# SiLU as one ScalarE function in a gated-DeltaNet layer, in place of a Tanh and a VectorE combination

## The chip, the cores and the metric

The program runs on one core of a Trainium2 chip. A core has five engines that run their own instruction streams and meet through semaphores: TensorE (PE, matrix products, with its weight loads shown as PEld), VectorE (DVE), ScalarE (ACT), GpSimd (POOL) and SyncE (SP, which issues the transfers). The metric is the device time of one execution in microseconds (us); the median of three runs stands for a kernel.

## The reference, cut to what matters

The program is a trunk of four layers on 256 frames of width 1024. The mixers are, in order, gated DeltaNet (GDN), mLSTM, differential attention, and GDN again; each is followed by a squared-ReLU MLP. So the part that is changed runs twice, in layer 0 and in layer 3. In the GDN mixer SiLU stands at two places:

```python
def gdn_mixer(h, w_in, conv_w, a_log, dt_bias, norm_g, w_out):
    proj = h @ w_in
    qkv = jax.nn.silu(causal_conv(proj[..., :GDN_QKV], conv_w))
    z = proj[..., GDN_QKV:GDN_QKV + GDN_HEADS * GDN_DV].reshape(b, t, GDN_HEADS, GDN_DV)
    ...
    q = l2_norm(qkv[..., :hk].reshape(b, t, GDN_HEADS, GDN_DK))
    k = l2_norm(qkv[..., hk:2 * hk].reshape(b, t, GDN_HEADS, GDN_DK))
    v = qkv[..., 2 * hk:].reshape(b, t, GDN_HEADS, GDN_DV)
    g = -jnp.exp(a_log) * jax.nn.softplus(a + dt_bias)
    beta = jax.nn.sigmoid(bt)
    o = gated_delta_rule(q, k, v, g, beta)
    o = rms_norm(o, norm_g) * jax.nn.silu(z)
    return o.reshape(b, t, GDN_HEADS * GDN_DV) @ w_out
```

The gated delta rule solves, for each head and each block of tokens, a lower triangular system whose matrix comes from the products of the keys and from decays exp(g_i - g_j).

## The kernel before

Products are done in two parts: each weight chunk is split into a high part (ACT copies it, L160) and a low part (DVE or POOL subtracts, L166), and each product is three matmuls. All products are recorded on one line, L174, so tiles are told apart by name. For the GDN layers POOL does the subtractions for the weights of q, v and z (`wlo_g`, `wlo_gz`) and of the output (`wlo_wo_g`), one piece of 128 x 1024 at a time.

A GDN layer goes through these stages. The keys are projected by token (`gkt`), transposed (`gp_1q`), convolved over four taps (L1033 on ACT for the last tap, L1039 on DVE for three) and given their SiLU, two heads at a time: q = 0 and 1 fill `gkT0`, q = 2 and 3 fill `gkT1`. The kernel holds twice the SiLU, y (1 + tanh(y / 2)): ACT computes the Tanh into a tile `cth` (L1041), DVE combines (L1042). Meanwhile the decays are made: ACT takes absolute differences (L1077) and an Exp in place (L1082) for half the heads at a time (`Eup0`, then `Eup1`), and POOL selects the triangles from them (L1083 into `L`, L1084 in place). Then come the Gram matrices of the keys (`gG`, on PE), their diagonals on DVE (L1099, the sums into `gck`), the scaling of `L` (L1108), and a copy of its diagonal blocks into `Lc` (L1112), once for each half of the heads. When both halves are there, DVE inverts all the blocks of 32 in a long chain of small products and subtractions (`LT` L1120, `Xt` L1130, `Xb` L1134) that ends in two transposes (`Xc` L1135, `Yc` L1136). PE takes `Yc` up at L1139 (`Za`) and builds larger inverses; the solve (`gw`), the state, the update of the right sides (`grhs`, L1234), attention and output follow. The values (`cy_2q`) and queries (`gqT`) have their convolution and SiLU at L1039 to L1044, and the gate (`zg`) its own at L990 and L991.

PE's order is written by hand in this part: blocks of projections (`gp`, `gz`) are issued between the chain's products for set amounts of time (the table `FILL`), and PE then runs in that order. The orders of the other engines come from a scheduler, which orders each engine's queue; a queue runs in order, so an instruction that waits holds up all that stand behind it on its engine. The tag `cvt` has four buffers, which the `cth`, `cy` and `diag` tiles share.

ScalarE's functions come in sets of tables, and an instruction that needs a function outside the loaded set is preceded in the program by an `ACT_TABLE_LOAD`. The program before has one, at its start.

Of the kernel before, what the change touches and what calls it, by code (L numbers as in the profile page):

```python
# [45 lines left out]
def shape_constants():  # L46
    """Arrays that depend on the shapes alone."""
# [6 lines left out]
    # [(b, d, n), j, r] is 1 at r = 2 j + d  # L54
# [12 lines left out]
def trunk_kernel(  # L67
# [33 lines left out]
    def bank(name):  # L101
        """for the wide products"""
        return ps_mm.tile([P, 512], F32, tag="mm", name=name)

    def tbank(name):
        """for transposes and the mixers' small products"""
        return ps_tr.tile([P, 512], F32, tag="tr", name=name)
# [23 lines left out]
    hold, hold_early = [], []  # L131
    # the latest instructions by name of the chain of norms between two sublayers
# [8 lines left out]
    def load_w(src, a, b, name, pool=(), early=(), chained=False, after=None):  # L141
        """A chunk of a weight matrix, [P, a, b]: get(part, k) is one of its two parts at k. The parts
        add up to the chunk, and each fits the matmul's reduced significand. The pieces in pool have GpSimd
        subtract; those in early lie where the sublayer before has left room. chained: the place of the pieces
        among the instructions of the chain, (0, 1) or (2, 3); after: what the subtractions follow."""
# [30 lines left out]
    def run(o, seq, start=True, stop=True, tail=0, name="T"):  # L176
        """tail: that many products at the end follow the transposes of the chain"""
        with ExitStack() as order:
            for i, (l, r) in enumerate(seq):
                if tail and i == len(seq) - tail:  # L180
                    order.enter_context(tc.issue_after(chain[name]))
                mm(o, l, r, start and i == 0, stop and i == len(seq) - 1)
# [4 lines left out]
    def load_g(row, name):  # L187
        """a row to all partitions"""
# [4 lines left out]
    def bc_g(g):  # L193
        """a row to all partitions by products with ones: at the start, the loads are what is waited for"""
# [37 lines left out]
    def rms_scale(ss, s):  # L232
        """for o = s * u per head with the sums of u * u given: s * rsqrt(mean(o * o) + eps), [P, 4]"""
# [8 lines left out]
    def mean_square(halves, junk):  # L242
        """sums of two halves' squares, scaled by 1 / sqrt(D) (a power of two) before squaring"""
# [44 lines left out]
    def steps(o, seq, tail=0):  # L288
        """the products of run() one by one, each with its cost in us"""
# [12 lines left out]
    def proj_tok(w, c0, hT, ts_, chunks, o, tail=0):  # L302
        """o[tokens of ts_, 512] = h @ w[:, c0:c0+512]"""
# [13 lines left out]
    def proj_ch(wt, ct, n, hT, o):  # L317
        """o[channels, T] for one tile of n channels of a chunk of columns"""
        run(o, ch_seq(wt, ct, n, hT))
# [5 lines left out]
    # blocks of products that fill PE's waits, by name and in order; each step issues some and gives their cost in us  # L325
    blocks = []

    def fill(us):
        """issue the blocks' products for that long"""
# [7 lines left out]
    def finish(key):  # L337
        """issue the blocks' products up to the end of that one"""
# [3 lines left out]
    def manual():  # L342
        """products run in the order in which they are issued"""
        return tc.manual_schedule(engines={mybir.EngineType.PE})

    def mixer_T(y, name, scale=None, alloc=bank):
        """a tile of the mixer's output by channel"""
# [5 lines left out]
    def out_steps(acc, oT, chunk, tail=None):  # L353
        """the output projection of a tile of tokens; tail: the products at the end follow that link of the chain"""
# [8 lines left out]
    def out_chunks(w, name, pool=(), after=None):  # L363
        """chunk(i): that part of the output weights, loaded when first asked for"""
# [9 lines left out]
    def finish_mixer(ys, chunk, name, scale=None, first=None, early_T=False):  # L374
        """x's update for each tile of tokens from the mixer's output by token (scaled by channel of a head).
        first: the first tile by channel; early_T: the second tile is there before the first one's products end"""
# [13 lines left out]
    def bc_cols(col):  # L390
        """a [P, 1] column as a [P, P] operand with equal columns"""
        return col.to_broadcast([P, P])

    def row_parts(parts, name, cols):
        """columns [P, (t, 8)] as rows, in two parts that add up: [(8 rows from 0 and from 32), T]"""
# [16 lines left out]
    def bc_rows(o, parts, h):  # L412
        """row h of the two parts' sum to all partitions of o"""
        mm(o, ident8[:, h : h + 1].to_broadcast([40, P]), parts, True, True)

    def log1p_exp_neg(ay, name):
        """log1p(exp(-ay)) for ay >= 0, as 2 atanh(e / (2 + e))"""
# [27 lines left out]
    def gate_cols(parts, hT, name, dst):  # L445
        """16 gate columns for all tokens: [P, NT, 16]"""
# [7 lines left out]
    def gate_steps(parts, hT, name, dst):  # L454
        """gate_cols(), with a stop after the products"""
# [100 lines left out]
    def diff(li, j, hT, first, second):  # L556
# [25 lines left out]
        def qk_block(s, hg, t, tail=0):  # L582
            """four heads of q (s=0) or k by token, scaled and turned"""
# [37 lines left out]
        def scores(hp, t):  # L621
            """the attention of heads 2hp, 2hp+1 for one tile of queries, but for the first map's 1 / sum"""
# [42 lines left out]
        def attend(hp, t):  # L665
            """the heads' outputs, with their RMS norm"""
# [103 lines left out]
    def mlstm(li, j, hT, first, second):  # L770
# [27 lines left out]
        # gates  # L798
# [43 lines left out]
        # q, k  # L842
# [9 lines left out]
        # output gate  # L852
# [90 lines left out]
    def gdn(li, j, hT, first, second):  # L943
# [21 lines left out]
        def k_block(hg, t, tail=0):  # L965
            """four heads of k by token, before the convolution"""
# [6 lines left out]
        def conv_block(s, q, alloc):  # L973
            """two heads of q (s=0) or v (2) by channel, before the convolution"""
# [9 lines left out]
        def z_block(hg, t):  # L984
# [5 lines left out]
            nc.scalar.activation(z_, ps, AF.Tanh, scale=0.5)  # L990
            nc.vector.scalar_tensor_tensor(z_, z_, 1.0, ps, op0=ALU.add, op1=ALU.mult)  # L991
# [7 lines left out]
        def gates():  # L999
# [19 lines left out]
            # gc holds minus the cumulative log decay  # L1019
# [8 lines left out]
        def conv(s, q, ps, dst):  # L1028
            """2 silu(conv) of channels of heads 2q, 2q+1, [P, 2, T], and the squares of q's"""
# [10 lines left out]
            th = cvt(f"cth_{li}_{s}{q}")  # L1040
            nc.scalar.activation(th, y, AF.Tanh, scale=0.5)  # L1041
            nc.vector.scalar_tensor_tensor(y, th, 1.0, y, op0=ALU.add, op1=ALU.mult)  # L1042
            if s == 0:
                nc.scalar.activation(th, y, AF.Square)  # L1044
                squares[q] = th
# [4 lines left out]
        def k_channels(q):  # L1050
            """heads 2q, 2q+1 of k by channel"""
# [7 lines left out]
        def square_sums(hg, dst):  # L1059
            """sums of squares over the channels of four heads of q by token: dst[:, t, h] + 4 EPS"""  # L1060
# [6 lines left out]
            nc.vector.tensor_scalar(dst, ps.rearrange("p (t h) -> p t h", h=4), 4 * EPS, None, op0=ALU.add)  # L1067

        def decays(hg, pr):
            """decays between tokens of a tile for two heads: below the diagonal (into L) and from it up"""  # L1070
# [16 lines left out]
        def grams(hg):  # L1087
            """L: the gram matrices of k, scaled, below the diagonal"""
# [12 lines left out]
            nc.vector.tensor_scalar(th8(ssk)[:, :, cols], th8(ssk)[:, :, cols], 4 * EPS, None, op0=ALU.add)  # L1101
# [12 lines left out]
            nc.vector.scalar_tensor_tensor(th8(c1)[:, :, cols], th8(rk)[:, :, cols], 0.5, th8(beta)[:, :, cols], op0=ALU.mult, op1=ALU.mult)  # L1114

        def base_inverse():
            """Xc: the inverses of the blocks in Lc, Yc: their transposes"""
            # the blocks' columns by lane: LT[(b, d, n), c, r] is block (b, n)'s at (r, c), and a lane of
            # Xb[(b, d, n), j, r] builds the inverse's columns 2 j + d
# [21 lines left out]
        def levels():  # L1141
            """the inverses' transposes Y from the blocks': pairs of blocks of 32, then of 64"""
# [363 lines left out]
```

## Time and profile before

| what | value |
|---|---|
| median of three runs | 1395.03 us |
| lowest and highest run | 1389.81 and 1833.45 us |
| span of the profiled execution, first to last instruction | 1386.8 us |
| that execution's own time beside its span | not given; the lowest run is 3.0 us above the span, the median 8.2 us |
| mean granted TensorE clock | 0.973 |

The profile is of one execution. Its page has the busy time of each engine, a row of 40 slices, the chain of work that ended last (followed back from the end, at each step to what released it) and the costliest groups of instructions. Beside the page the trace answers questions: who waited for whom, the instructions of one engine in order of time (merged where neighbours are alike; a bracket at a row's end is the idle time before it and what ended that), the chain in a window, and all the instructions of one line or one tile. In a group's row stand the count, the busy time and the mean in ns.

### The profile page before, as it was taken

To read this page: it belongs to the slowest core of one execution; us is meant where nothing else is said; L and a number is where in the kernel's file an instruction comes from. 1 tells how busy PE (TensorE), PEld (TensorE's weight loads), DVE (VectorE), ACT (ScalarE), POOL (GpSimd) and SP (SyncE) were. 2 spreads that over 40 slices of the span, in tenths; PEclk is the share of its full clock that TensorE was granted. 3 is DMA by queue.
4 is the path that set the end of the run, shared out by engine and by line. 5 is a ranking of instruction groups with operands and counts; after the bars stand their busy time and mean duration, and the time that the engine had idled before them with its cause. 6 is when DMAs were issued, how large, how long until landed. Compare 5 with 4: busy or idle time off the path is not lost.

```text
span 1386.8 us, 20876 instructions
## 1 busy us (share of the span) xinstructions
PE 1309.9 (94%) x8010; PEld 1138.4 (82%) x8010; DVE 897.1 (65%) x1525; ACT 710.4 (51%) x1215; POOL 245.9 (18%) x225
## 2 busy tenths in 40 slices
PE   8875999999999999999999999999999498999998
PEld 6774878898888888989877788989878487899896
DVE  6897668555575786555555576555579965865452
ACT  6634656444454555444465655444464385554441
POOL 3682240000010110000032110000057426000000
PEclk9996999999999999999999999999999799999999
DMA  8351137565655256565463157555463313466550
GB/s 277 107 181 62 47 137 243 183 191 186 203 166 184 88 177 222 185 186 195 136 214 122 63 187 237 182 183 187 150 204 92 122 47 122 155 208 188 181 192 34
DMA packets 131627, 222.77 MB, mean 161 GB/s; under 512 B 10883, under 2 KB 81093, under 8 KB 131526
## 3 DMA queue, kind: packets, MB, share of 16 engines
q1 hardware_dynamic: 131524, 221.42, 49.7%
q8 instruction: 63, 1.03, 0.3%
q14 instruction: 38, 0.31, 0.1%
q10 hardware_dynamic: 2, 0.00, 0.0%
HBM read 220.35 MB, written 1.05 MB: 160 GB/s over the span
## 4 chain that ended last, share of the span: by engine, by line
PE 79%; DVE 15%; DMA 2%; ACT 2%; issue 1%; POOL 1%; SPq 0%; DVEq 0%; POOLq 0%; ACTq 0%
PE acc_mlp L174 26%; PE mmc L174 20%; PE mmt L174 6%; DVE Lc L1112 3%; PE acc_wo_g L174 2%; PE gz L174 2%; DVE Xt L1130 2%; PE dq L174 2%; PE dv L174 2%; PE mo L174 2%; PE acc_wo_m L174 2%; PE acc_wo_d L174 2%; PE mqk L174 2%; DVE Xb L1134 2%; PE mv L174 1%
## 5 line engine op out<-in xcount | busy, mean ns | idle before, releaser
L166 DVE TENSOR_TENSOR wlo_w<-raw_w,whi_w 128x1024 fp32r<-128x1024 f32 x256 | 307.2, 1223 | 217.3 <-ACT whi_w L160 216.6
L160 ACT ACTIVATE whi_w<-raw_w 128x1024 fp32r<-128x1024 f32 x256 | 264.3, 1056 | 220.4 <-PE mmc L174 103.9
L174 PE MATMUL acc_mlp<-whi_w,aThi 128*128 128x512 f32 x512 | 203.1, 397 | 0.0
L174 PE MATMUL acc_mlp<-whi_w,aTlo 128*128 128x512 f32 x512 | 202.7, 396 | 0.0
L174 PE MATMUL acc_mlp<-wlo_w,aThi 128*128 128x512 f32 x512 | 202.6, 396 | 0.0
L139 POOL TENSOR_TENSOR rr<-ms,mhalf 128x1 f32<-128x1 f32 x32 | 17.4, 544 | 604.7 <-DVE ms L251 604.7
L174 PEld LDWEIGHTS acc_mlp<-wlo_w,aThi 128*128 128x128 f32 x512 | 96.5, 188 | 23.1
L174 PEld LDWEIGHTS acc_mlp<-whi_w,aThi 128*128 128x128 f32 x512 | 96.5, 189 | 21.8
L174 PEld LDWEIGHTS acc_mlp<-whi_w,aTlo 128*128 128x128 f32 x512 | 96.5, 188 | 21.8
L174 PE MATMUL mmc<-hThi,wlo_w 128*128 128x256 f32 x768 | 108.8, 284 | 0.0
L174 PE MATMUL mmc<-hTlo,whi_w 128*128 128x256 f32 x768 | 107.8, 283 | 0.0
L174 PE MATMUL mmc<-hThi,whi_w 128*128 128x256 f32 x768 | 107.7, 283 | 0.0
L174 PEld LDWEIGHTS mmc<-hThi,whi_w 128*128 128x128 f32 x768 | 100.0, 191 | 1.8
L174 PEld LDWEIGHTS mmc<-hThi,wlo_w 128*128 128x128 f32 x768 | 99.3, 192 | 0.0
L174 PEld LDWEIGHTS mmc<-hTlo,whi_w 128*128 128x128 f32 x768 | 99.0, 192 | 0.0
L166 POOL TENSOR_TENSOR wlo_g<-raw_g,whi_g 128x1024 fp32r<-128x1024 f32 x32 | 76.7, 2424 | 34.4 <-ACT whi_g L160 29.3
L524 ACT ACTIVATE aThi<-rc 128x512 fp32r<-128x512 f32 x48 | 30.3, 632 | 78.3 <-DVE rc L522 78.3
L525 DVE TENSOR_TENSOR aTlo<-rc,aThi 128x512 fp32r<-128x512 f32 x48 | 33.2, 692 | 32.6 <-ACT aThi L524 32.6
L166 POOL TENSOR_TENSOR wlo_wo_g<-raw_wo_g,whi_wo_g 128x1024 fp32r<-128x1024 f32 x16 | 38.1, 2406 | 49.4 <-ACT whi_wo_g L160 48.3
L166 POOL TENSOR_TENSOR wlo_gz<-raw_gz,whi_gz 128x1024 fp32r<-128x1024 f32 x16 | 38.0, 2400 | 48.0 <-ACT whi_gz L160 48.0
L174 PE MATMUL gp<-hThi,whi_g 128*128 128x256 f32 x256 | 40.2, 303 | 5.8 <-DVE gck L1101 5.8
L225 ACT ACTIVATE hThi<-T_pre 128x512 fp32r<-128x512 f32 x32 | 17.4, 594 | 50.2 <-PE T_pre L220 50.2
(419 smaller groups left out, 2598.7 us busy)
## 6 DMA issues: line engine op xcount, KB each, us to landing
raw_w<-in_mlp_w_dram SPq DMA_DIRECT2D x256, 512.0 KB, 4.1
raw_g<-in_gdn_w_in_dram SPq DMA_DIRECT2D x32, 512.0 KB, 3.9
raw_gk<-in_gdn_w_in_dram SPq DMA_DIRECT2D x16, 512.0 KB, 4.9
raw_gz<-in_gdn_w_in_dram SPq DMA_DIRECT2D x16, 512.0 KB, 3.7
raw_wo_g<-in_gdn_w_out_dram SPq DMA_DIRECT2D x16, 512.0 KB, 3.2
raw_d<-in_diff_w_in_dram SPq DMA_DIRECT2D x16, 512.0 KB, 4.6
gpost<-in_norm_g_dram SPq DMA_DIRECT2D x8, 512.0 KB, 4.6
raw_mv<-in_mlstm_w_in_dram SPq DMA_DIRECT2D x8, 512.0 KB, 4.7
```

The lines of the kernel that those rows point to most:

```text
L139: return nc.gpsimd.tensor_tensor(dst, src, m, op=ALU.pow)
L160: nc.scalar.activation(hi, raw, AF.Copy)
L166: eng.tensor_tensor(lo, raw, hi.bitcast(F32), op=ALU.subtract)
L174: nc.tensor.matmul(o, l, r, start=start, stop=stop)
L225: a = nc.scalar.activation(hs, ps3, AF.Copy)
L524: nc.scalar.activation(hs, r, AF.Copy)
L525: nc.vector.tensor_tensor(aTs[j][1][:, 2 * q : 2 * q + 2, :].rearrange("p a b -> p (a b)"), r, hs.bitcast(F32), op=ALU.subtract)
L1112: nc.vector.tensor_copy(Lc[bs, hg * 8 : hg * 8 + 8, :], src)
L1130: nc.vector.tensor_tensor(t3, LT[:, c : c + 1, rs].to_broadcast([P, m, r1 - r0]), Xb[:, :m, c : c + 1].to_broadcast([P, m, r1 - r0]), op=A ...
L1134: nc.vector.tensor_tensor(Xb[:, :m, rs], Xb[:, :m, rs], t3, op=ALU.subtract)
```

## The change

In `conv`, the Tanh on ACT and the combination on DVE are replaced by one ACT instruction, Silu, in place; the squares of q get a tile of their own, since the Tanh's tile that they reused is gone. The gate's Tanh and combination become one Silu from PSUM. As the values are now the SiLU and not twice it, three factors go: the epsilon in the sums of squares is no longer multiplied by four, and the halves in `c1` and in the gain are dropped.

```diff
 def z_block(hg, t):
     ...
-            nc.scalar.activation(z_, ps, AF.Tanh, scale=0.5)
-            nc.vector.scalar_tensor_tensor(z_, z_, 1.0, ps, op0=ALU.add, op1=ALU.mult)
+            nc.scalar.activation(z_, ps, AF.Silu)
 ...
 def conv(s, q, ps, dst):
     ...
-            th = cvt(f"cth_{li}_{s}{q}")
-            nc.scalar.activation(th, y, AF.Tanh, scale=0.5)
-            nc.vector.scalar_tensor_tensor(y, th, 1.0, y, op0=ALU.add, op1=ALU.mult)
+            nc.scalar.activation(y, y, AF.Silu)
             if s == 0:
-                nc.scalar.activation(th, y, AF.Square)
-                squares[q] = th
+                squares[q] = cvt(f"csq_{li}_{q}")
+                nc.scalar.activation(squares[q], y, AF.Square)
             return y
 ...
-            nc.vector.tensor_scalar(dst, ps.rearrange("p (t h) -> p t h", h=4), 4 * EPS, None, op0=ALU.add)
+            nc.vector.tensor_scalar(dst, ps.rearrange("p (t h) -> p t h", h=4), EPS, None, op0=ALU.add)
 ...
-            nc.vector.scalar_tensor_tensor(th8(c1)[:, :, cols], th8(rk)[:, :, cols], 0.5, th8(beta)[:, :, cols], op0=ALU.mult, op1=ALU.mult)
+            nc.vector.tensor_tensor(th8(c1)[:, :, cols], th8(rk)[:, :, cols], th8(beta)[:, :, cols], op=ALU.mult)
 ...
-        ghalf = sm("ghalf", 1)
-        nc.vector.tensor_scalar(ghalf, cw[:, 96:97], 0.5, None, op0=ALU.mult)
+        gain = sm("gain", 1)
+        nc.vector.tensor_copy(gain, cw[:, 96:97])
```

Silu and Exp are not in one set of tables, so the program after has twelve table loads where it had one: five in each GDN layer and one in the mLSTM layer, ahead of its first Exp (L420). Line numbers are one lower after the change from L992 to L1040 and three lower from L1044 on. The scheduler also orders some queues anew; POOL's and SP's orders are the same in both programs, and PE's but for two neighbouring products.

ScalarE, layer 0, where the second half of the keys and the decays are made (`cth_0_12` and `cth_0_13` are the Tanh tiles of `gkT1`, `Eup0` and `Eup1` the decays of the two halves of the heads, `whi_g0_..` copies of weights, `cy_0_20` the first values). Before:

```order
L1077 ACTIVATE Eup1_0_502<-gcb_0_10_585,ngc_113 128x128 x4
L1082 ACTIVATE Eup0_0_500<-Eup0_0_500 128x512 x2
L1077 ACTIVATE Eup1_0_502<-gcb_0_11_594,ngc_113 128x128 x4
L160 ACTIVATE whi_g0_00_0_888<-raw_g0_00_0_886 128x1024
L160 ACTIVATE whi_g0_00_1_894<-raw_g0_00_1_892 128x1024
L1041 ACTIVATE cth_0_12_533<-gkT1_0_441 128x512
L1041 ACTIVATE cth_0_13_544<-gkT1_0_441 128x512
L1082 ACTIVATE Eup1_0_502<-Eup1_0_502 128x512 x2
L1033 ACTIVATE cy_0_20_668<-gp_0_20_498,cw_0_290 128x256 x2
```

The same place after:

```order
L1074 ACTIVATE Eup1_0_498<-gcb_0_10_577,ngc_113 128x128 x4
L1079 ACT_TABLE_LOAD
L1079 ACTIVATE Eup0_0_496<-Eup0_0_496 128x512 x2
L1074 ACTIVATE Eup1_0_498<-gcb_0_11_586,ngc_113 128x128 x4
L160 ACTIVATE whi_g0_00_0_878<-raw_g0_00_0_876 128x1024
L160 ACTIVATE whi_g0_00_1_884<-raw_g0_00_1_882 128x1024
L1039 ACT_TABLE_LOAD
L1039 ACTIVATE gkT1_0_441<-gkT1_0_441 128x512 x2
L1079 ACT_TABLE_LOAD
L1079 ACTIVATE Eup1_0_498<-Eup1_0_498 128x512 x2
L1032 ACTIVATE cy_0_20_660<-gp_0_20_494,cw_0_290 128x256 x2
```

The order of the work is the same; three loads stand between it. One more stands ahead of the Silu of `gkT0`, further up, and a fifth ahead of the Silu of `cy_0_20`, further down, behind which the next copies of weights stand.

VectorE, layer 0, around the copy of the first half's blocks into `Lc`. Before:

```order
L1042 SCALAR_TENSOR_TENSOR gkT1_0_441<-cth_0_13_544,gkT1_0_441 128x512
L1108 SCALAR_TENSOR_TENSOR L0_0_501<-gG_0_00_633,gc2_120,L0_0_501 128x128 x4
L1108 SCALAR_TENSOR_TENSOR L0_0_501<-gG_0_01_642,gc2_120,L0_0_501 128x128 x4
L1114 SCALAR_TENSOR_TENSOR gc1_119<-grk_118,beta_111 128x2x4
L1039 SCALAR_TENSOR_TENSOR cy_0_20_668<-gp_0_20_498,cw_0_290,cy_0_20_668 128x255
L1099 SCALAR_TENSOR_TENSOR diag_0_632,gck_116<-gG_0_10_714,csq_98 128x128 x2
L1112 COPY Lc_0_625<-L0_0_501 32x256 x4
```

After:

```order
L1105 SCALAR_TENSOR_TENSOR L0_0_497<-gG_0_01_634,gc2_120,L0_0_497 128x128 x4
L1111 TENSOR_TENSOR gc1_119<-grk_118,beta_111 128x2x4
L1038 SCALAR_TENSOR_TENSOR cy_0_20_660<-gp_0_20_494,cw_0_290,cy_0_20_660 128x255
L1109 COPY Lc_0_617<-L0_0_497 32x256 x4
L1038 SCALAR_TENSOR_TENSOR cy_0_20_660<-gp_0_20_494,cw_0_290,cy_0_20_660 128x254
L1096 SCALAR_TENSOR_TENSOR diag_0_624,gck_116<-gG_0_10_704,csq_98 128x128 x2
```

The combinations are gone, and two diagonals of the second half have moved from ahead of the copy to behind it; the first product of `cy_0_20` still stands ahead of it.

VectorE, layer 0, at the update of the right sides (`grhs11`, which the second half's solve reads). Before:

```order
L1234 SCALAR_TENSOR_TENSOR grhs10_0_883<-gKS_0_0_1594,gnc2e_121,grhs10_0_883 128x128 x4
L1039 SCALAR_TENSOR_TENSOR gqT0_0_880<-gp_0_01_1096,cw_0_290,gqT0_0_880 128x253
L1039 SCALAR_TENSOR_TENSOR gqT1_0_881<-gp_0_02_1145,cw_0_290,gqT1_0_881 128x253
L991 SCALAR_TENSOR_TENSOR zg_0_0_878<-zg_0_0_878,gz_0_10_1526 128x512
L1042 SCALAR_TENSOR_TENSOR gqT0_0_880<-cth_0_01_1674,gqT0_0_880 128x512
L1042 SCALAR_TENSOR_TENSOR gqT1_0_881<-cth_0_02_1686,gqT1_0_881 128x512
L1234 SCALAR_TENSOR_TENSOR grhs11_0_885<-gKS_0_1_1631,gnc2e_121,grhs11_0_885 128x128 x4
```

After:

```order
L1038 SCALAR_TENSOR_TENSOR gqT0_0_870<-gp_0_01_1086,cw_0_290,gqT0_0_870 128x253
L1231 SCALAR_TENSOR_TENSOR grhs10_0_873<-gKS_0_0_1577,gnc2e_121,grhs10_0_873 128x128 x4
L1038 SCALAR_TENSOR_TENSOR gqT1_0_871<-gp_0_02_1135,cw_0_290,gqT1_0_871 128x253
L1231 SCALAR_TENSOR_TENSOR grhs11_0_875<-gKS_0_1_1613,gnc2e_121,grhs11_0_875 128x128 x4
L1239 TENSOR_TENSOR Eup0_0_496<-Eup0_0_496,gP_0_00_1680 128x512
```

The combinations of the gate and of two pairs of queries no longer stand ahead of the second update.

More of the change, by code (lines that the diff above doesn't have):

```diff
@@ L1100, in grams @@
                                                    accum_out=ssk[:, c : c + 1])
-            nc.vector.tensor_scalar(th8(ssk)[:, :, cols], th8(ssk)[:, :, cols], 4 * EPS, None, op0=ALU.add)
+            nc.vector.tensor_scalar(th8(ssk)[:, :, cols], th8(ssk)[:, :, cols], EPS, None, op0=ALU.add)
             nc.vector.reciprocal(th8(rk2)[:, :, cols], th8(ssk)[:, :, cols])
@@ L1439, in gdn @@
                 fill(F[25])
-                oT = mixer_T(zg[0], f"wo_g{li}0", ghalf, tbank)
+                oT = mixer_T(zg[0], f"wo_g{li}0", gain, tbank)
                 finish("z11")
@@ L1444, in gdn @@
         yield
-        yield from finish_mixer(zg, out_chunks(gdn_w_out[j], f"wo_g{li}", Z_POOL), f"wo_g{li}", ghalf, oT, True)
+        yield from finish_mixer(zg, out_chunks(gdn_w_out[j], f"wo_g{li}", Z_POOL), f"wo_g{li}", gain, oT, True)
     kinds = {"gdn": gdn, "mlstm": mlstm, "diff": diff}
```

## The prediction

> **What bounds the kernel now.** I read the page's span first, then PE's waits in the two GDN layers, then the chain in layer 0, and then POOL, DVE and ACT in order of time along that chain. The change touches nothing outside the GDN layers but one table load.
>
> ```profile
> span 1386.8 us, 20876 instructions
> ...
> PE Za L1139 <- DVE Yc L1136: 20.4, 1, 20.4
> PE gw L174 <- DVE grhs L1234: 1.3, 1, 1.3
> PE acc_wo_g L174 <- DVE oTlo_wo_g L229: 0.7, 1, 0.7
> ...
> PE Za L1139 <- DVE Yc L1136: 19.1, 1, 19.1
> PE gw L174 <- DVE grhs L1234: 2.8, 1, 2.8
> ...
> 120.04:215.00 94.96, 91.32 (x705) 79.03 (x706) 61.97 (x129) 62.19 (x147) 35.59 (x23) 0.96 0.28 95
> ```
>
> The waits are those of layer 0 and then of layer 3. In each layer PE runs out of work and stands some 20 us until DVE has written `Yc`. So a us by which `Yc` comes later or sooner is a us of the span. After `Yc`, PE is busy 91.3 of 95 us (the last row: length, then busy time of PE first), so there only PE's own small waits count.
>
> What sets `Yc`? The chain in layer 0 (start, length, what):
>
> ```profile
> 62.90 0.39 DVE cy L1039
> 63.29 0.42 DVE diag L1099 x4
> 63.71 11.46 DVE Lc L1112
> ...
> 103.43 0.21 DVE Xb L1134 x2
> ...
> 119.90 0.14 issue
> 120.04 0.23 PE Za L1139
> ```
>
> POOL beside it in order of time, and then the COPYs into `Lc` (all sixteen by shortest, median and longest in ns; the second group of layer 0; the first of layer 3):
>
> ```profile
> 59.33 1.65 POOL L139 TENSOR_TENSOR grk<-gck,mhalf 128x8 f32<-128x8 f32 x1 [2.00 <-DVE gck L1101]
> 60.94 0.63 POOL L1083 TENSOR_SCALAR_AFFINE_SELECT L<-Eup 128x512 f32<-128x512 f32 x1
> 61.52 1.84 POOL L1366 MEMSET Y<- 128x1024 f32 x2
> 65.55 9.46 POOL L166 TENSOR_TENSOR wlo_g<-raw_g,whi_g 128x1024 fp32r<-128x1024 f32 x4
> 79.56 1.65 POOL L139 TENSOR_TENSOR grk<-gck,mhalf 128x8 f32<-128x8 f32 x1 [4.54 <-DVE gck L1101]
> 81.88 9.72 POOL L166 TENSOR_TENSOR wlo_g<-raw_g,whi_g 128x1024 fp32r<-128x1024 f32 x4 [0.66 <-ACT whi_g L160]
> 91.56 11.84 POOL L166 TENSOR_TENSOR wlo_gz<-raw_gz,whi_gz 128x1024 fp32r<-128x1024 f32 x5
> ...
> L1112 DVE COPY Lc<-L x16: 273/1338/11527, 63.6 to 1076.7; 32x256 f32<-32x256 f32 x16
> 84.24 7.51 DVE L1112 COPY Lc<-L 32x256 f32<-32x256 f32 x4
> 1050.98 12.43 DVE L1112 COPY Lc<-L 32x256 f32<-32x256 f32 x4
> ```
>
> A COPY into `Lc` takes 0.27 us at best and 11.53 us at worst. The worst one starts at 63.6, while POOL clears and selects, and ends at 75.2, just after POOL's four subtractions (65.55 + 9.46 = 75.01). In layer 3 the same group takes 12.43 us. So POOL holds DVE up, and here until POOL has nothing left. In POOL's second run (81.88 to 91.56 + 11.84 = 103.40) the COPYs and the first steps of the inversion get in one per subtraction: four COPYs take 7.51. From 103.4 on DVE runs free, 16.5 us to `Yc` (119.9). So `Yc` is the end of POOL's second run plus 16.5, and that run starts when ACT has made its weights.
>
> At the first hold the Trainium skill (SBUF — State Buffer, Who interferes with whom) says that the shared port pair is an exclusive lock, held for a whole instruction by the one that issued first; by that a COPY would wait for one POOL instruction. The second run agrees (2.4 us a COPY), the first does not: 11.5 us, past seven POOL instructions.
>
> **The change, part by part.** ACT's rows, then DVE's removed groups:
>
> ```profile
> 1.36 1.28 ACT L246 ACT_TABLE_LOAD   x1 [1.36 <-PEq L1493]
> 3.50 0.63 ACT L246 ACTIVATE h_pre<-x 128x512 f32<-128x512 f32 x1 [0.86 <-DMA x<-in_x_dram]
> ...
> 58.14 1.20 ACT L1041 ACTIVATE cth<-gkT 128x512 f32<-128x512 f32 x2
> 59.18 1.19 ACT L1082 ACTIVATE Eup<-Eup 128x512 f32<-128x512 f32 x2
> 60.22 0.88 ACT L1033 ACTIVATE cy<-gp,cw 128x256 f32<-128x256 f32 x2
> 79.50 0.63 ACT L1041 ACTIVATE cth<-cy 128x512 f32<-128x512 f32 x1 [13.41 <-DVE gck L1101]
> ...
> L1042 DVE SCALAR_TENSOR_TENSOR gqT<-cth,gqT 128x512 f32<-128x512 f32 x8 | 11.0, 1397 | 1.9 <-ACT cth L1041 1.9
> L1042 DVE SCALAR_TENSOR_TENSOR gkT<-cth,gkT 128x512 f32<-128x512 f32 x8 | 9.6, 1221 | 1.5 <-ACT cth L1041 1.5
> L1042 DVE SCALAR_TENSOR_TENSOR cy<-cth,cy 128x512 f32<-128x512 f32 x8 | 6.6, 824 | 19.2 <-ACT cth L1041 19.2
> ```
>
> *Silu for Tanh.* Tanh (two in 1.20) and Exp (two in 1.19) of this size cost the same, and Tanh alone 0.63; I take Silu as Tanh, a change of 0. No row shows Silu; were one 0.1 dearer or cheaper, the four ahead of POOL's select would move it by 0.4 either way.
>
> *A table load, c.* The one load took 1.28. Two neighbours of 0.65 take 1.19, so they overlap by about 0.1, which a load between them loses: c = 1.4. From below 1.28. From above: after the load ACT stood 0.86 for a transfer, and a stall hidden in that would not show, so 1.28 + 0.86 + 0.1, about 2.2. I take 1.4, nearest the load's own row. The Trainium skill (ScalarE: Activation LUTs, What ACT_TABLE_LOAD costs) gives each switch 1.28 us of load and 1.38 of drain, 2.66; the first figure agrees with the row, the second no row shows, and with it my sum below would be +20 in place of +8.
>
> *Four loads ahead of the second Exp pair, in each GDN layer.* ACT has no idle time from 48 to 60 us, so the loads add up: 4 x 1.4 = 5.6. The first Exp of the pair ended at 59.85 (59.18 + 0.67), but POOL began its select only at 60.94, held by its power until 60.98: 1.1 us of cover. The select and the memsets and subtractions behind it move by 5.6 - 1.1 = +4.5.
>
> *The COPY.* It stands behind a product of `cy`, which needs ACT's Copy behind the Exps: it arrives some 1.5 us after the first Exp (0.5 for the second Exp, 0.5 for the Copy, 0.4 for the product), which is in POOL's memsets (0.6 to 2.4 us after the select starts). That is the state in which it was held before, so I let it be held again, to POOL's last subtraction: +4.5. The two diagonals moved behind it add 0.4 (the 0.42 row). The two combinations ahead of it and the one behind it save nothing: POOL is what DVE waits for.
>
> *The fifth load* stands ahead of the Silu of `cy_20`, for which ACT waited 13.4 us, and ahead of the copies that POOL's second run needs: + c = 1.4. DVE comes to that run with a lead that it had not (about 2 us, the load and a removed combination), gets two or three more steps in, and has that much less to do free: -0.5.
>
> So `Yc` moves by 5c - 1.1 + 0.4 - 0.5 = 5c - 1.2 = +5.8 in a layer, and +11.6 in both.
>
> *After `Yc`.* The other combinations (queries, part of the values, the gate) lie beside PE's work. These rows are where they do not:
>
> ```profile
> 155.88 3.06 DVE L1042 SCALAR_TENSOR_TENSOR gqT<-cth,gqT 128x512 f32<-128x512 f32 x2 [1.25 <-ACT cth L1041]
> 1142.43 5.23 DVE L1042 SCALAR_TENSOR_TENSOR gqT<-cth,gqT 128x512 f32<-128x512 f32 x2 [0.70 <-ACT cth L1041]
> 192.78 3.49 DVE L166 TENSOR_TENSOR wlo_w<-raw_w,whi_w 128x1024 fp32r<-128x1024 f32 x3
> ...
> L811 DVE SCALAR_TENSOR_TENSOR lf<-gt,lp_p x1: 169/169/169, 432.9 to 432.9; 128x16 f32<-128x16 f32 x1
> L174 PE MATMUL mF<-lf,csq x4: 173/256/257, 435.7 to 436.2; 128*128 128x8 f32 x4
> ```
>
> The two pairs stood ahead of `grhs11`; without them PE's waits of 1.3 and 2.8 go. In layer 0 `oTlo_wo_g` no longer stands behind the third of three `wlo_w` (3.49 together), and PE's wait of 0.7 goes. That is -4.8 at most; at worst the queries' Silu, now ahead of other work on ACT, holds the same PE products, and it is 0. I take -4.0.
>
> *The twelfth load* (mLSTM, L420) delays `lf`, ready at 433.1, by 1.4; PE reads it at 435.7, so 2.6 us cover it. Beyond that it would cost its excess. The constants, the smaller tile count and the copy for the gain cost nothing: small instructions in the place of equal ones.
>
> Sum: 2 x 5.8 - 4.0 = +7.6 us, or 10c - 6.4. The profiled span becomes 1394.4. The runs shown lie 3.0 (lowest) to 8.2 (median) above the span; with the middle, 5.6, I forecast 1400.0 us. With c from 1.28 to 2.2, the last term from -4.8 to 0 and 3.0 to 8.2 around the span, the likeliest case has 1395 to 1415.
>
> **The rivals.** *The hold breaks.* If the COPY gets in between two memsets, as later ones get in between subtractions, DVE is done with the second half early, POOL goes from the subtractions (75.0 + 4.5 = 79.5) straight through its power (1.65) into its second run at 81.15, 0.7 before now; with 0.3 for more steps done, -1.0 a layer, and with -4.0 it is -6: 1386.4. For it speaks that every later COPY got in; against it that at 63.6 the COPY passed memset, select and subtraction without getting in, in both layers.
>
> *The load stalls for longer than it shows.* With c = 2.2, the sum is +15.6: 1408. Only one load stands in the trace, with ACT idle behind it.
>
> *Slower by over 2%* (27.9 us, about what a measurement of this kernel can tell from no change): the same mechanism, at the same place, decides from 10c - 6.4 = 27.9, that is c = 3.4. Against it: that is 2.5 times the row.
>
> *The removed work counts in full.* If DVE's own work set every stage and the loads were hidden, the three groups (27.2) and the waits (4.8) would go: -32, 1360. Against it: most of that work lies after `Yc`, beside a PE that is 96% busy, and the part before it lies in POOL's shadow. That the change does nothing is excluded by the loads in the program's order.
>
> **How the numbers follow.** Held COPY at c near 1.4: 0.60. The hold breaks: 0.20. A longer stall: 0.14. Over 2% slower: 0.04. Removed work in full: 0.02. The time is that of the first, 1400. The range reaches to the broken hold less 2 for its waits (1384) and to the longer stall with the full time around the span (1416), and leaves out 0.06 and the tails. Faster by over 2%: 0.02; within 2%: 0.94; slower: 0.04.
>
> **What would show it.** Right: eleven new loads of about 1.3 us; POOL's select of the second half some 4.5 us later after the keys' convolution; one COPY of over 10 us in each GDN layer; PE's waits up to `Yc`, summed, 5 to 6 us longer in each layer; no waits of PE for `grhs`. Wrong: four short COPYs (the hold broke), ACT idle beside the loads (a stall), a `Yc` no later than before although the COPY was held, or new waits of PE behind `Yc`, for the queries' Silu or for `gz`.

## The result and the profile after

The changed kernel takes 1378.5 us (median of four runs, 1375.0 to 1380.4), where the kernel before takes 1394.2. The ratio is 0.9903, with a 95% interval from 0.9879 to 0.9927: faster by 13.5 us, where 7.6 us slower was forecast (the ratio is of the fast runs, without the one of 1833 us). The time lies outside the range, on the other side of no change.

PE's waits in layer 0 (first three) and in layer 3, from the list of who waited for whom (in total, times, longest), and PE's work after `Yc` in layer 0 (length, then busy time of PE; the last figure but two is the granted clock):

```profile
PE Za L1136 <- DVE Yc L1133: 18.5, 1, 18.5
...
PE gkt L174 <- DVE gain L1303: 1.5, 1, 1.5
PE gv L1196 <- ACT kd L1189: 1.3, 1, 1.3
...
PE Za L1136 <- DVE Yc L1133: 19.7, 1, 19.7
...
119.44:215.00 95.56, 93.89 (x727) 81.62 (x728) 56.42 (x123) 63.69 (x148) 37.93 (x24) 0.98 0.35 111
```

The waits for `grhs` and `oTlo_wo_g` are gone, as forecast, and so are those of `gp` for `gck` (2.6 and 3.2 before). The loads, on ACT in layer 0 in order of time:

```profile
50.84 0.58 ACT L971 ACTIVATE gkt<-gkt 128x512 f32<-128x512 f32 x1
51.44 1.28 ACT L1039 ACT_TABLE_LOAD   x1
52.73 1.15 ACT L1039 ACTIVATE gkT<-gkT 128x512 f32<-128x512 f32 x2
...
58.45 1.28 ACT L1079 ACT_TABLE_LOAD   x1
59.74 1.15 ACT L1079 ACTIVATE Eup<-Eup 128x512 f32<-128x512 f32 x2
...
63.83 1.28 ACT L1039 ACT_TABLE_LOAD   x1
65.12 1.15 ACT L1039 ACTIVATE gkT<-gkT 128x512 f32<-128x512 f32 x2
66.29 1.28 ACT L1079 ACT_TABLE_LOAD   x1
67.59 1.15 ACT L1079 ACTIVATE Eup<-Eup 128x512 f32<-128x512 f32 x2
```

Each load takes 1.28 us, the next instruction starts 0.01 after it, and the overlap of about 0.1 between neighbours is lost: 1.39. Two Silus take 1.15, as two Exps do. No stall is to be seen behind any of these loads.

What the forecast had otherwise is POOL and VectorE at the second half's decays, layer 0 (for VectorE the first COPY's group, and all sixteen COPYs by shortest, median and longest in ns):

```profile
68.29 0.63 POOL L1080 TENSOR_SCALAR_AFFINE_SELECT L<-Eup 128x512 f32<-128x512 f32 x1 [3.42 <-ACT Eup L1079]
68.87 1.85 POOL L1363 MEMSET Y<- 128x1024 f32 x2
70.65 0.51 POOL L1366 MEMSET X<- 32x512 f32 x1
71.13 0.67 POOL L1080 TENSOR_SCALAR_AFFINE_SELECT L<-Eup 128x512 f32<-128x512 f32 x1
71.76 1.31 POOL L1081 TENSOR_SCALAR_AFFINE_SELECT Eup<-Eup 128x512 f32<-128x512 f32 x2
73.05 9.53 POOL L166 TENSOR_TENSOR wlo_g<-raw_g,whi_g 128x1024 fp32r<-128x1024 f32 x4
82.54 1.65 POOL L139 TENSOR_TENSOR grk<-gck,mhalf 128x8 f32<-128x8 f32 x1
84.16 9.51 POOL L166 TENSOR_TENSOR wlo_g<-raw_g,whi_g 128x1024 fp32r<-128x1024 f32 x4
93.63 9.36 POOL L166 TENSOR_TENSOR wlo_gz<-raw_gz,whi_gz 128x1024 fp32r<-128x1024 f32 x4
...
69.90 3.33 DVE L1109 COPY Lc<-L 32x256 f32<-32x256 f32 x4
...
L1109 DVE COPY Lc<-L x16: 282/476/1417, 69.9 to 1065.3; 32x256 f32<-32x256 f32 x16
```

The longest COPY is 1.42 us, where it was 11.53: the hold, in which the first COPY waited for the end of POOL's unbroken run of instructions, broke, in both layers. The first COPY waits from 69.90 to the end of the MEMSET of `X`, gets in ahead of the select at 71.13, and the others get in one per select. The second half's work, which before waited for POOL's four subtractions, now runs beside them; POOL comes to its second run without a wait (before 4.5 us ahead of its power and 0.66 ahead of the run), has one subtraction fewer in it (eight against nine), and VectorE enters it with all COPYs done. The ninth is missing for another reason than the hold: in the new program ACT's copy of that piece of the gate's weights stands behind ACT's copy of the inversion's `Xc` (it came at 98.68 before and comes at 123.28 now), so POOL subtracts it after `Yc`, at 124.42.

The two profiled spans differ by less (1386.8 and 1377.6) than the runs do. Matching PE's 8010 products one by one gives the difference from the kernel before at each:

```
product                               before    after   difference
layer 0, gc_r (ahead of Silu)          45.87    48.57     +2.70
layer 0, Za (behind Yc)               120.04   119.44     -0.60
layer 0, gw (behind grhs)             160.03   156.88     -3.15
layer 0, mmt (MLP, behind the mixer)  210.78   206.57     -4.21
layer 1, acc_wo_m                     490.78   485.85     -4.93
layer 2, dq                           744.67   743.23     -1.44
layer 3, gp                          1024.03  1023.47     -0.56
layer 3, gc_r (ahead of Silu)        1032.05  1029.62     -2.43
layer 3, Za                          1107.15  1101.20     -5.95
layer 3, gw (behind grhs)            1148.75  1139.64     -9.10
layer 3, mmt (MLP, behind the mixer) 1196.84  1187.61     -9.22
```

The +2.70 stands there ahead of the first Silu; at this place executions differ by as much (the traces below have `gc_r` anywhere from 44.81, in `b_gap`, to 49.34, in `a_ktanh_ozf`). The loss in layer 2, which the change does not touch, is the granted clock (the last figure but two) in this one execution; the same 17 products before and after:

```profile
741.00:745.00 4.00, 4.00 (x17) 2.12 (x16) 1.56 (x4) 2.48 (x9) 1.70 (x6) 0.99 0.01 2
...
736.00:743.00 7.00, 7.00 (x17) 3.40 (x16) 1.25 (x4) 2.53 (x9) 1.70 (x6) 0.50 0.01 4
```

The gain from -0.56 to -2.43 at the head of layer 3 is the clock too, the other way round: 0.66 before (1027 to 1032) and 1.00 after (1026.5 to 1030).

So in the changed layers: from `gc_r` up to `Yc` -3.3 (layer 0, from +2.70 to -0.60) and -3.5 (layer 3, from -2.43 to -5.95), from there to the MLP -3.6 and -3.3. Together -13.7, within the interval of the runs (-10.2 to -16.9). Of the gain up to `Yc`, 0.4 and 0.9 are an earlier start of POOL's second run, and 2.7 in each layer are its length (21.5 before, 18.8 after), nearly all of it the subtraction that is missing. So what the broken hold saves is little more than what the loads cost.

### The profile page after: what moved, and what is told of

Its sections match the earlier page's. It is cut to its first block, busy times and chain, and to the rows that moved or that the text cites. A ratio compares the mean times of both kernels' runs of the same rounds, so it can differ in the third digit from the quotient of the medians.

```text
span 1377.6 us, 20856 instructions
## 1 busy us (share of the span) xinstructions
PE 1308.7 (95%) x8010; PEld 1135.3 (82%) x8010; DVE 850.9 (62%) x1493; ACT 725.0 (53%) x1226; POOL 244.6 (18%) x225
## 4 chain that ended last, share of the span: by engine, by line
PE 81%; DVE 11%; ACT 3%; DMA 2%; issue 1%; POOL 1%; SPq 0%; DVEq 0%; POOLq 0%; ACTq 0%
PE acc_mlp L174 26%; PE mmc L174 20%; PE mmt L174 6%; PE acc_wo_g L174 3%; PE gz L174 3%; DVE Xb L1131 2%; DVE Xt L1127 2%; PE dq L174 2%; PE dv L174 2%; PE mo L174 2%; PE acc_wo_d L174 2%; PE acc_wo_m L174 2%; PE mqk L174 2%; PE gp L174 2%; PE acc_S L174 2%
## 5 line engine op out<-in xcount | busy, mean ns | idle before, releaser
L160 ACT ACTIVATE whi_g<-raw_g 128x1024 fp32r<-128x1024 f32 x32 | 33.3, 1059 | 15.4 <-DMA raw_g<-in_gdn_w_in_dram 11.6
```

The costliest lines, as they stand in the source:

```text
L160: nc.scalar.activation(hi, raw, AF.Copy)
```

## The experiments

My theory after the result: the hold broke since the COPY came at another moment of POOL's run, and that made the change faster. Rivals: what stands right in front of the COPY on VectorE (before, the accumulating diagonals) makes the hold; or the loads on ScalarE broke it by drawing POOL's two halves apart. The ratios below are to the kernel before on the same chip (median 1388 to 1389 us there).

### The kernel before with the diagonals behind the COPYs (b_order)

```diff
+                        if hg:
+                            order.enter_context(tc.issue_after(copies[0]))
                         nc.vector.scalar_tensor_tensor(junk, G[t][:, h * P : (h + 1) * P], 1.0, ident, ...
```

> The kernel before (Tanh and combination), with one thing of the change: in both GDN layers the two diagonals of the second half's gram stand behind the four COPYs into Lc on VectorE, so that the first COPY follows the convolution's product and comes 0.42 us sooner, into the second MEMSET of Y in place of the MEMSET of X. Theory 'neighbour' (an accumulating diagonal right in front of the COPY makes the hold): four short COPYs. Theory 'arrival' (a COPY that comes in the MEMSET of X is held to the end of POOL's run, one that comes earlier gets in): four short COPYs. Rival 'ScalarE's delay' (the hold broke because the table loads came between POOL's two halves): the COPY takes 11.5 us as before. If it breaks, POOL's second run starts right after its power, some 5 us sooner, in each layer: 1383 us against 1393; if it holds, 1393.

Measured: 0.9935 (0.9915 to 0.9956), 9.0 us faster, without any Silu. POOL and the COPY:

```profile
64.75 2.67 DVE L1117 COPY Lc<-L 32x256 f32<-32x256 f32 x4
...
64.84 0.52 POOL L1374 MEMSET X<- 32x512 f32 x1
65.32 0.68 POOL L1083 TENSOR_SCALAR_AFFINE_SELECT L<-Eup 128x512 f32<-128x512 f32 x1
```

Four COPYs in 2.67 us. The hold breaks without loads, so the loads are not needed for it. POOL's second run keeps its nine subtractions in both layers, so this gain is the hold's alone: 9.0 us are to be had in the kernel before by moving two small instructions.

### Where the COPY comes, and what stands in front of it (b_pad, a_pad)

```diff
+            for i in range(pads):
+                pad = nc.vector.scalar_tensor_tensor(diag[:, ...], G[1][:, 3 * P :], 1.0, ident, op0=ALU.mult, op1=ALU.mult).ins
             for b in range(NB):
```

Shown is the padding alone. The first kernel, `b_pad`, also keeps the COPYs behind the last pad and, in layer 0, the diagonals behind the first COPY. The second, `a_pad`, is the changed kernel with the diagonals ahead of the COPY again in layer 0 and five pads in layer 3.

> The kernel before with plain products (no accumulation) as padding on VectorE. Layer 0: the diagonals behind the COPYs, one pad ahead, so that the COPY follows a convolution's product and comes about 0.2 us into the MEMSET of X. Layer 3: three pads, two of them ahead of the convolution's product and one right in front of the COPY, the diagonals behind: the COPY comes in the select behind the MEMSET of X. 'Neighbour': short COPYs in both layers. 'Arrival': a COPY of about 11 us in layer 0, and in layer 3 too if what counts is to have missed the MEMSETs of Y. 'ScalarE's delay': 11 us in both.

> The changed kernel (Silu) with the COPY moved later on VectorE. Layer 0: one more product and the two diagonals ahead of the COPY, as in the kernel before: it follows an accumulating diagonal, and comes at the start of the MEMSET of X. Layer 3: three padding products and one more of the convolution ahead: it follows a plain product and comes about 0.4 us into the MEMSET of X. 'Neighbour': held (10 us or more) in layer 0, short in layer 3. 'Arrival': held in both. 'ScalarE's delay': short in both.

Measured, the first one in layer 0 and layer 3 (COPYs, then the MEMSET of `X` and the select behind it), and the second one in layer 0 and layer 3:

```profile
65.00 2.47 DVE L1123 COPY Lc<-L 32x256 f32<-32x256 f32 x4
...
64.89 0.52 POOL L1380 MEMSET X<- 32x512 f32 x1
65.37 0.68 POOL L1083 TENSOR_SCALAR_AFFINE_SELECT L<-Eup 128x512 f32<-128x512 f32 x1
...
1046.28 11.97 DVE L1123 COPY Lc<-L 32x256 f32<-32x256 f32 x3
...
1046.26 0.63 POOL L1083 TENSOR_SCALAR_AFFINE_SELECT L<-Eup 128x512 f32<-128x512 f32 x1
...
69.98 12.57 DVE L1120 COPY Lc<-L 32x256 f32<-32x256 f32 x4
...
70.29 0.63 POOL L1080 TENSOR_SCALAR_AFFINE_SELECT L<-Eup 128x512 f32<-128x512 f32 x1
...
1058.65 12.55 DVE L1120 COPY Lc<-L 32x256 f32<-32x256 f32 x4
...
1058.90 0.63 POOL L1080 TENSOR_SCALAR_AFFINE_SELECT L<-Eup 128x512 f32<-128x512 f32 x1
```

The neighbour falls: behind a plain product the COPY is held too (1046.28, 1058.65). ScalarE's delay falls: with Silu and all its loads the COPY is held again (69.98, 1058.65). My 'arrival' holds, but for one place: in layer 0 of the first kernel the COPY came 0.11 us into the MEMSET of `X` and got in. How long it has waited when the select behind that MEMSET starts tells the cases apart. By the starts of the single instructions in the five kernels so far:

```
kernel, layer                    waited before the select   the COPY took
changed kernel, 0 and 3              1.23, 1.24 us             1.42, 1.42
b_order, 0 and 3                     0.57, 0.57                0.75, 0.75
b_pad, 0                             0.37                      0.55
a_pad, 0 and 3                       0.31, 0.25               11.68, 11.65
kernel before, 0 and 3               0.14, 0.14               11.53, 11.53
b_pad, 3                            -0.03                     11.38
```

The border lies between 0.31 and 0.37 us, and the traces of the later kernels agree (0.14 held in `a_ktanh` and `b_gap`, 0.56 to 1.24 let in, in four more). The MEMSET of `X` takes 0.48 up to the select in all of them, so the COPY's place in that MEMSET (let in when it came 0.11 us after its start, held from 0.17 on) tells the cases apart just as well. No run separates the two readings.

The second kernel, the changed one with the hold back, took 1395.1 us in its one execution, 7.3 over the kernel before (with some five extra products of VectorE in layer 3, about 0.24 each). That this is near the forecast's +7.6 is in part luck. Product by product, against the trace before, `Yc` comes 2.3 us later in layer 0, where the ninth subtraction is missing from POOL's run again, and 4.9 later in layer 3, where it is not; behind `Yc` 3.0 and 1.8 come back. That is +2.3 in the changed layers, and most of the rest stood there ahead of the first Silu (1.9) or came in layer 2 (3.2). Against the changed kernel's -13.7 in the same count, the hold's return costs some 16 us, and the ninth subtraction in layer 3 is a part of that.

### A gap in POOL's run (b_gap)

```diff
                     sel = nc.gpsimd.affine_select(e, e, [[0, 4], [1, P]], ALU.is_ge, 0.0, base=0, channel_multiplier=-1)
+                if hg == 1:
+                    gap = sm("gap", 8)
+                    with tc.issue_after(sel.ins):
+                        sel = nc.gpsimd.tensor_tensor(gap, ones.to_broadcast([P, 8]), mhalf[:, :8], op=ALU.pow)
```

> The kernel before with one more small power on POOL (128x8, an unused result) between the second half's last select and the first of the four subtractions, in both GDN layers. In the traces VectorE's instructions run freely beside POOL's power. Theory 'unbroken run' (a COPY that has missed the boundary ahead of the select is held as long as POOL's large instructions follow one another without a gap): the first COPY comes in the MEMSET of X as before, but ends with the power's start, after some 2.2 us in place of 11.5. Rival 'to the last subtraction' (the COPY waits for what POOL has queued, whatever stands between): 13 us.

```profile
62.58 2.98 DVE L1116 COPY Lc<-L 32x256 f32<-32x256 f32 x4
...
68.81 6.83 DVE L1105 TENSOR_SCALAR gck<-gck 128x8 f32<-128x8 f32 x1
...
64.49 1.68 POOL L1088 TENSOR_TENSOR gap<-ones,mhalf 128x8 f32<-128x8 f32 x1
66.14 9.47 POOL L166 TENSOR_TENSOR wlo_g<-raw_g,whi_g 128x1024 fp32r<-128x1024 f32 x4
75.73 1.64 POOL L139 TENSOR_TENSOR grk<-gck,mhalf 128x8 f32<-128x8 f32 x1
```

The first COPY comes as late as before (0.14 us ahead of the select) and ends 0.17 after the power's start, after 2.08 us; the others run beside the power. So a held instruction waits for the end of POOL's unbroken run. Layer 3 has the same 2.08 and 0.17. The second line shows that the hold is not the COPY's own: a `gck` of 128x8 that comes inside the four subtractions is held for 6.83, to their end. 1377.8 us in one execution; the ninth subtraction is out of POOL's second run here too, so not all of that is the hold.

### Tanh for the keys alone (a_ktanh)

```diff
+            if s == 1:
+                th = cvt(f"cth_{li}_{s}{q}")
+                nc.scalar.activation(th, y, AF.Tanh, scale=0.5)
+                nc.vector.scalar_tensor_tensor(y, th, 1.0, y, op0=ALU.add, op1=ALU.mult)
+            else:
+                nc.scalar.activation(y, y, AF.Silu)
```

> The changed kernel with Tanh and the combination kept for the keys alone; values, queries and gate have Silu. The loads ahead of the second half's Exp go, and VectorE has the diagonals ahead of the COPY again. Theory 'the hold decides': the COPY is held for 10 us or more in both layers, and the time is within 4 us of the kernel before, above the changed kernel, although it has three table loads in a layer fewer (ratio 0.997 to 1.000). Rival 'fewer loads and less of VectorE's work decide': at least as fast as the changed kernel (ratio 0.990 or lower).

Measured: 0.9973 (0.9953 to 0.9992). The longest COPY:

```profile
L1114 DVE COPY Lc<-L x16: 281/284/11548, 65.8 to 1069.8; 32x256 f32<-32x256 f32 x16
```

With three table loads in the program behind the first in place of eleven, and the gate, the values and the queries on Silu, it is slower than the changed kernel, since VectorE's order and with it the hold (11.55 and 11.53) are those of before. The ninth subtraction is out of POOL's run in both, so the hold decides between these two.

### The gate's subtractions on VectorE after Yc (a_z_dve, b_order_z, a_ktanh_oz)

If POOL's runs set `Yc`, work that POOL need not do there should go. The gate's weights are needed after `Yc`:

```diff
-                zck[hg] = tok_chunks(w, 3 * hk + hg * 512, f"gz{li}_{hg}", (0, 1, 2, 3))
+                zck[hg] = tok_chunks(w, 3 * hk + hg * 512, f"gz{li}_{hg}", ())
```

> The changed kernel with the eight subtractions of the gate's weights on VectorE after Yc, in place of POOL before it. If POOL's run sets Yc, the run before it has four subtractions in place of eight, and Yc comes some 8 us sooner in each layer; VectorE gets 8 x 1.2 us more after Yc, where it has room: 1362 to 1368 us. If PE, or the queries' weights, set Yc's neighbourhood: 1378 or more.

> The kernel before, without Silu, with the diagonals behind the COPYs and the gate's subtractions on VectorE after Yc. The hold's 9 us and the subtractions' 8: about 1370 us on a chip with 1388 for the kernel before; less, if the gate's combinations and subtractions on VectorE do not get in each other's way after Yc; more, up to 1380, if they do. Beside the run with Tanh for the keys alone it tells what Silu for values, queries and gate is worth when the hold is away.

> The same (Tanh for the keys alone), with the diagonals behind the COPYs, and with the gate's subtractions on VectorE after Yc. The hold broken, POOL's run 4 to 5 us sooner than in the changed kernel for want of the loads, eight subtractions out of the way: 1355 to 1362 us on a chip with 1388 for the kernel before, 4 to 10 us under the changed kernel with the gate's subtractions moved. If the loads cost nothing on the path: 1364 to 1368.

Measured: 0.9845 (0.9823 to 0.9866) for the changed kernel with it, 8 us under the changed kernel, near the weak end of what was expected (`Za` 9.5 us sooner in layer 0, of which 3.3 are given back up to the MLP, 1.5 of them where `gz` now waits for ACT's copy `gq`). 0.9838 (0.9803 to 0.9872) for the kernel before with it and with the diagonals behind: 1363.7 us, where about 1370 was expected. 0.9791 (0.9769 to 0.9812) for the last, 1358.6 us, the fastest version here: 2.1% under the kernel before, 1.1% under the changed one. PE's waits for `Yc` in it:

```profile
PE Za L1146 <- DVE Yc L1143: 7.7, 1, 7.7
...
PE Za L1146 <- DVE Yc L1143: 9.0, 1, 9.0
```

The last two differ by Silu for gate, values and queries: 0.47% or 6.5 us for it, with intervals that overlap a little. The first and the last differ mainly by Silu for the keys: 0.54% or 7.5 us against it, for eight loads in the program, less the keys' combinations.

### The loads alone (a_ktanh_ozl)

```diff
                 nc.vector.scalar_tensor_tensor(y, th, 1.0, y, op0=ALU.add, op1=ALU.mult)
+                if q % 2:
+                    switch[q // 2] = nc.scalar.activation(sm("switch", 1), th[:, 1, :1], AF.Silu).ins
 ...
+                    with tc.issue_after(switch[hg]):
                         nc.scalar.activation(e, e, AF.Exp, scale=-1.0)
```

> The version with Tanh for the keys, diagonals behind the COPYs and the gate's subtractions moved, plus one Silu of 128x1 (unused result) between the keys' Tanh and the Exps of each half: eight more table loads in the program, at the places at which the changed kernel has them, and nothing else. No COPY of over 3 us. If a load costs its duration and the lost overlap on the path to Yc (1.3 to 1.4, times four in a layer, less about 1 that lies in the cover ahead of POOL's select): 7 to 10 us over the version without (ratio 0.984 to 0.987 to the kernel before). If a load stalls ScalarE for 2.7: 18 us over it (0.992). If the loads are covered: no more than 2 over it (0.979 to 0.981).

Measured: 0.9897 (0.9868 to 0.9925), 14.7 us over the version without, more than the 7 to 10 expected. The interval reaches to the 0.992 of a stall, so the trace has to decide. In layer 0:

```profile
69.25 2.26 DVE L1123 COPY Lc<-L 32x256 f32<-32x256 f32 x4
...
75.18 8.95 DVE L1112 TENSOR_SCALAR gck<-gck 128x8 f32<-128x8 f32 x1
...
72.83 0.62 POOL L1089 TENSOR_SCALAR_AFFINE_SELECT L<-Eup 128x512 f32<-128x512 f32 x1
...
74.61 9.49 POOL L166 TENSOR_TENSOR wlo_g<-raw_g,whi_g 128x1024 fp32r<-128x1024 f32 x4
```

The COPYs now come so early, ahead of the delayed run, that they are done when the select starts, no request of VectorE waits there, and the next one, `gck`, is held to the run's end: 8.95 us, and 10.3 in layer 3. Counted from `gc_r`, POOL's select comes 5.5 us later than in the version without in layer 0, which is four loads and two small Silus (4 x 1.28 + 2 x 0.20), and 4.1 later in layer 3; `Za` comes 8.8 and 7.1 later. The 3 us beyond the select's delay I put down to the hold; no run has these loads without it. A load by itself stalls nothing: behind each, ACT goes on after 0.01 us (but for the first of the program, where it waits for a transfer).

### More work for PE ahead of Za (a_ktanh_ozf)

```diff
-    (0.7, 0.7, 0.2, 2.7, 1.1, 1, 3.6, 23.2, ...
+    (0.7, 0.7, 0.2, 2.7, 1.1, 1, 3.6, 26.6, ...
```

The same in layer 3, 21.4 to 24.8.

> The same version without the extra loads, and with 3.4 us more of the queries' and the gate's products given to PE ahead of Za in both GDN layers (they need the gate's first parts only). PE stands 7.7 and 9.0 us ahead of Za there; if those products are ready, 3 us of each wait are filled: ratio 0.975 to 0.977. If what PE is given ahead of Za is missing later, or its weights come late: 0.979 or more.

Measured: 1.0096 (1.007 to 1.0122), a loss of 42 us against the version without. PE's largest waits in layer 0, and ACT there:

```profile
PE gP L174 <- ACT gqT L1044: 9.9, 2, 6.9
PE gp L174 <- ACT gq L982: 8.3, 1, 8.3
...
105.74 0.63 ACT L1162 ACTIVATE X<-Xc 32x512 f32<-32x512 f32 x1 [10.82 <-DVE Xc L1142]
106.28 0.57 ACT L982 ACTIVATE gq<-gp 128x512 f32<-128x512 f32 x1
```

The products added need a bank that ACT's copy `gq` frees, and that copy stands on ACT behind one that waits for the end of the inversion. PE, whose order is fixed, waits for it ahead of `Za`, and the queries come late after that.

## Why the prediction was wrong

**The step that failed** is the one called *The COPY*: it put the COPY's arrival 1.5 us after the select's start, into POOL's memsets, and went on "That is the state in which it was held before, so I let it be held again". The arrival was right (69.90 is 1.61 after 68.29). The state was not that of before: there the COPY came 2.70 after the select (60.94 to 63.64), in the MEMSET of `X`, 0.14 us ahead of the next select. The rows of before:

```profile
63.30 0.51 POOL L1369 MEMSET X<- 32x512 f32 x1
63.77 0.63 POOL L1083 TENSOR_SCALAR_AFFINE_SELECT L<-Eup 128x512 f32<-128x512 f32 x1
...
63.64 12.43 DVE L1112 COPY Lc<-L 32x256 f32<-32x256 f32 x4
```

The two arrivals, 1.5 and 2.70, lay in the prediction's own numbers; by these the old one stood behind the span that it gave as the memsets' (0.6 to 2.4). The step read 'in the memsets' as one state, where the last 0.3 to 0.4 us divides it in two. The runs put in its place: a COPY that has waited 0.37 us or more when the select starts gets in, one of 0.31 or less waits to the end of the run. With the hold put back into the changed kernel its gain was gone (7.3 over before in one execution, +2.3 in the changed layers).

**The rival 'the hold breaks'** had the mechanism, at 0.20, but was too small, -6 against -13.5. It took `Yc` 1.0 sooner in a layer, 0.7 of it for POOL's earlier second run, and that run did start 0.4 and 0.9 sooner; but `Yc` came 3.3 and 3.5 sooner, since the run also lost its ninth subtraction (some 2.4). Neither the forecast nor the rival looked at the place of that copy in ACT's new order. So of the 21 us between the forecast's +7.6 and the measured -13.5, the step named above is some 13.6 (+5.8 against the rival's -1.0, in two layers), the subtraction 4.8, and the work after `Yc` 2.9.

**After `Yc`**, taken at -4.0 with -4.8 as the bound, -6.9 came. The waits named (4.8) all went. Some 1.1 more came with the clock in layer 0, in the work right behind `Za` (before, then after):

```profile
120.04:135.00 14.96, 14.93 (x225) 13.54 (x225) 6.46 (x13) 12.11 (x25) 7.10 (x3) 0.76 0.22 69
...
119.44:134.00 14.56, 14.53 (x236) 13.12 (x237) 6.84 (x18) 13.62 (x28) 9.45 (x4) 0.84 0.33 106
```

PE was granted 0.84 against 0.76. The rest, about 1.0, I did not follow.

**What held.** The load: c = 1.39 against 1.4; twelve of twelve rows have 1.28. Silu costs what Tanh costs. POOL's select came 4.7 us later in layer 0 (68.29 - 60.94, less the 2.70 at `gc_r`) and 4.2 in layer 3 (1050.06 - 1048.28, and the 2.43 there), against 4.5. From the end of POOL's second run to `Za` it was 16.5 us in both layers, much as before (16.6 and 16.3). The mLSTM layer's load cost nothing that shows. The 'longer stall' and the price of 2.66 us a switch (the Trainium skill, ScalarE: Activation LUTs, What ACT_TABLE_LOAD costs) find no row: the instruction behind a load starts 0.01 us after it. The rule of the lock (the Trainium skill, SBUF — State Buffer, Who interferes with whom) agrees with the turns taken in a run that VectorE entered in time, and not with the holds, which last over seven instructions.

**The time around the span** was 1.7 us in the profiled execution after, where 5.6 was taken. The range's upper end counted it twice: 1386.8 + 15.6 + 8.2 is 1410.6, and 1416 is that with 5.6 more. Neither changes the outcome.

## What to carry to other kernels

Where two engines share a resource, an instruction's cost can depend on its moment by tenths of a us: a forecast that moves either engine must place the arrival against the border, and price both sides, before it lets a hold stand. Look for small instructions that can be put behind a contended one; here two diagonals were worth 0.65%. Changing the function of an engine that switches tables in a chain costs each switch there, 1.39 us here, less what cover stands ahead; where the queue has no switch nearby (gate, values, queries) it seems to pay (6.5 us, with intervals that overlap a little). And look through every queue's new order for work that has moved across the chain: here one copy on ACT took a subtraction of 2.4 us out of POOL's run.

## What the runs showed of the hardware

A VectorE instruction that uses SBUF (a COPY, a TENSOR_SCALAR of 128x8) and meets an unbroken run of POOL's selects and subtractions is either let in at the boundaries, one per POOL instruction, or held to the run's end: 6.8 to 11.7 us in eleven cases. A power of 128x8 on POOL (1.65 us) ended the hold in both layers of `b_gap`, and COPYs took their 0.28 beside it. In the second half's selects and the four subtractions behind them, in every trace, the run was open when a request of VectorE had waited 0.37 us or longer at the start of the select behind the MEMSET of `X`, and closed otherwise. Whether the waiting or the place in the MEMSET counts was not tried, and whether that is the whole rule is open: in the second run of the kernel before (from 81.88) `gnc2e` came 0.83 us after the start and got in at the first boundary, and the COPYs behind it took turns. What differs there was not tried.

The convolution's products into `cy`, which read PSUM, took 0.47 to 0.48 us beside POOL's subtractions, in every trace; with POOL idle they took 0.44 to 0.48.
